# A higher queue priority for the attention steps of the second layer, on ScalarE and VectorE

## The chip, the cores and the metric

The kernel runs on one core of one Trainium2 chip. The time is the device time of one execution in microseconds (us). Three runs of the kernel before gave 984.35, 983.63 and 985.03, with a median of 984.35. The engines are named as in the profile: PE (TensorE matmul), PEld (its weight loads), DVE (VectorE), ACT (ScalarE), POOL (GpSimd), SP (SyncE, which issues most DMAs).

## The reference

A decoder trunk of two layers works on 16 learned meta tokens and 512 tokens of width 1024. The first layer is gated linear attention. The second layer, in which the change lies, is differential softmax attention with 8 heads. All is in float32. Cut to what matters:

```python
def diff_branch(xn, w_in, lam_vecs, gnorm, w_out, rel_table, lambda_init):
    proj = xn @ w_in                                  # 1024 -> 4 * 2048
    q, k, v, z = jnp.split(proj, 4, axis=-1)
    ...
    def block(args):                                  # 128 queries, all heads
        s = jnp.einsum('bhpqd,bhpkd->bhpqk', qb, kh) * scale + bias[None, :, None]
        s = jnp.where(dist >= 0, s, -jnp.inf)
        p = jax.nn.softmax(s, axis=-1)
        a = p[:, :, 0] - lam * p[:, :, 1]             # two softmaxes per head
        return jnp.einsum('bhqk,bhkv->bhqv', a, vh)
    ...
    o = head_rms(o) * gnorm.astype(f32) * (1.0 - lambda_init)
    y = jax.nn.silu(z.astype(f32)) * o.reshape(B, L, D_INNER)
    return (y.astype(xn.dtype) @ w_out)
```

After both layers a final RMS norm is taken and the meta tokens are dropped.

## The kernel before

**Precision.** Every float32 product is made of three matmuls of a shortened type: high times high, high times low, low times high. So each operand is split: `split` lets ACT copy the value into the shortened type (line 269, the high part), and DVE subtract that from the value (line 270, the low part). Weights come from DRAM into tiles called `raw` and are split into `wh`, `wl`.

**Projection units.** For queries, keys, values and gates of a head the weights are taken in 2 x 2 blocks, and a `Unit` multiplies with sums of blocks, so that fewer products are needed. Its block weights are `a11h`, `a11l`, `a12h` and so on, its sums of weights `sum` (line 356). Each product goes into one of the PSUM banks `bx`, `bv`, `by` (line 421, `product`). The first product and one in the middle are evacuated by ACT into a tile `u` (line 442, `partial`); later products are added to `u` by DVE into `t` (lines 467 and 469, `add`). There are two banks `bx` and one each of the others: until `u` or `t` has emptied a bank, PE cannot begin the product that takes it next.

**Attention of a head.** `diff_steps` returns four steps, each for one of four blocks of 128 queries. `scores` makes the two score products on PE (line 390), adds the bias tile `T` on DVE and keeps the minimum of the negated scores (line 1635), takes the exponentials on ACT (line 1637, tile `p`) and joins the two softmaxes on DVE (lines 1640 to 1642). `turn` transposes the result on PE and splits it into `aT` and, for the 16 meta keys, `am` (ACT lines 269, 397, 398; DVE lines 270, 400). `values` multiplies with the values on PE (lines 390 and 1666) and takes the head's RMS norm: ACT (lines 1670, 1671), a power on POOL (line 1673), ACT again (line 1674, tile `on`). `rows` transposes that on PE (line 1680), multiplies with the gate on DVE (line 1683, tile `yt`) and splits it into `hT`.

Values must be reversed in token order: `leave` copies them into `planes` (line 579), sends them to DRAM (line 580), and transposing DMAs on SP bring them back (lines 588, 590).

**What sets the order.** PE's list is written out by hand: the whole kernel is under a manual schedule for PE, so PE's instructions run in the order of the code. In the second layer the code is a loop over heads and steps; after each step a planner `W` fills in pieces of projection units for the next head until a share of their time is used up. So the code's order interleaves one head's attention with the next head's projections. For ACT, DVE and SP a scheduler builds the lists: among the instructions it holds ready in its own model, the one of the highest priority goes first. The priority follows the place in the code; `high_priority(offset=...)` moves an instruction ahead as if it stood that many places earlier. The helper `urgent` gives 100 to what it wraps: the four attention steps, `partial`, `add`, `gate` (lines 1514 to 1516) and `leave`. Splits of weights have no such offset.

Of the kernel before, what the change touches and what calls it, by code (L numbers as in the profile page):

```python
# [208 lines left out]
def trunk(ctx, tc, x, meta, g_norm, gla_w_in, gla_w_gate_up, gla_b_gate, gla_gnorm, gla_w_out,  # L209
# [21 lines left out]
    def T(p, shape, dt, tag, **kw):  # L231
        uid[0] += 1
        return p.tile(shape, dt, tag=tag, name=f"{tag}_{uid[0]}", **kw)
# [10 lines left out]
    def ps_tile():  # L244
        return T(ps_pool, [P, 512], F32, "ps")
# [4 lines left out]
    def h2(t):  # L250
        return t.rearrange("p (a b) -> p a b", a=2)

    def urgent(fn):

        def run(*a, **kw):
            with tc.high_priority(offset=100):
                return fn(*a, **kw)
        return run


    kept = []

    def split(hi, lo, src, scale=None, keep=False):

        if keep:
            act.activation(hi, src, AF.Copy)
            kept.append(lambda: dve.tensor_tensor(lo, src, hi.bitcast(F32), op=ALU.subtract))
        elif scale is None:
            act.activation(hi, src, AF.Copy)  # L269
            dve.tensor_tensor(lo, src, hi.bitcast(F32), op=ALU.subtract)  # L270
        else:
            act.activation(hi, src, AF.Copy, scale=scale)
            dve.scalar_tensor_tensor(lo, src, scale, hi.bitcast(F32), op0=ALU.mult, op1=ALU.subtract)
# [112 lines left out]
    def mm3(ps, a, b, first=True, last=True, **kw):  # L386

        pairs = ((a[0], b[0]), (a[0], b[1]), (a[1], b[0]))
        for n, (l, r) in enumerate(pairs):
            pe.matmul(ps, l, r, start=first and n == 0, stop=last and n == 2, **kw)  # L390

    def split3(dst, src, lo, scale=None):


        kw = {} if scale is None else {"scale": scale}
        hi = dst[:32].bitcast(F32)
        act.activation(dst[:32], src, AF.Copy, **kw)
        act.activation(dst[96 - lo:128 - lo], src, AF.Copy, **kw)
        if scale is None:
            dve.tensor_tensor(dst[lo:lo + 32], src, hi, op=ALU.subtract)  # L400
        else:
            dve.scalar_tensor_tensor(dst[lo:lo + 32], src, scale, hi, op0=ALU.mult, op1=ALU.subtract)
# [873 lines left out]
    pf = ps_tile()  # L1276
    pe.matmul(pf[0:1, 0:1], fl[:, 1:2], one1, start=True, stop=True)
    told = urgent(dve.tensor_copy)(fi, pf[0:1, 0:1])
    with tc.issue_after(told.ins):
        token_sums(4)  # L1280
# [68 lines left out]
    def boundary(m):  # L1349
        urgent(split)(xs2[0][m], xs2[1][m], hT[:, m, :], scale=g_sb[:, 1, m:m + 1])  # L1350
        if m >= 4:
            squares2(m)

        def post():
            if m == 0:
                bd.pm = ps_tile()
            pt = ps_tile()
            for b in range(4):
                pe.transpose(pt[:, b * P:(b + 1) * P], hT[:, m, NM + b * P:NM + (b + 1) * P], ident)
            if m < 4:  # L1360
                pe.transpose(bd.pm[:NM, m * P:(m + 1) * P], hT[:, m, :NM], ident)
            act.activation(hacc[:, :, m * P:(m + 1) * P], pt.rearrange("p (b c) -> p b c", b=4), AF.Copy)
            if m == 3:
                for b in range(5):
                    n = BLK[b][1]
                    t = hacc[:, b - 1, :512] if b else bd.pm[:NM, :]
                    act.activation(tmp()[:n, :512], t, AF.Square, accum_out=sums[:n, b:b + 1])
        W.defer(2.6, post)
        if m == KT - 1:
            W.defer(2.8, norm_sums)  # L1370
# [66 lines left out]
    for i in range(2):  # L1437
        urgent(dve.tensor_tensor)(z0r[:, i, :], z0[i], rb[:, NM:], op=ALU.mult)
# [179 lines left out]
    def diff_steps(hd, s, ys):  # L1618


        @urgent
        def scores(b):
            r = Head()
            r.nk = nk = NM + P * (b + 1)
            r.ta, r.b = b * P, b
            r.st = st = T(ep, [P, 8], F32, "st", bufs=4)
            r.p = []
            ko = L - nk
            for m in range(2):
                p = T(ep, [P, L], F32, "p", bufs=3)  # L1630
                for c0, c1 in ([(0, nk)] if nk <= 512 else [(0, HT), (HT, L)]):
                    ps = ps_tile()
                    mm3(ps[:, :c1 - c0], [s.q[j][:, m, r.ta:r.ta + P] for j in range(2)],
                        [s.k[j][:, m, ko + c0:ko + c1] for j in range(2)])
                    dve.tensor_tensor_reduce(p[:, c0:c1], ps[:, :c1 - c0], s.T[:, c0:c1], op0=ALU.add, op1=ALU.min, scale=1.0,  # L1635
                                             scalar=st[:, m:m + 1] if c0 else 1.0e38, accum_out=st[:, m:m + 1])
                act.activation(p[:, :nk], p[:, :nk], AF.Exp, scale=-1.0, bias=st[:, m:m + 1], accum_out=st[:, 2 + m:3 + m])  # L1637
                r.p.append(p[:, :nk])

            dve.reciprocal(st[:, 5:6], st[:, 3:4])  # L1640
            dve.scalar_tensor_tensor(st[:, 5:6], st[:, 5:6], lam, st[:, 2:3], op0=ALU.mult, op1=ALU.mult)
            dve.scalar_tensor_tensor(r.p[0], r.p[1], st[:, 5:6], r.p[0], op0=ALU.mult, op1=ALU.subtract)
            return r

        @urgent
        def turn(r):
            b, a = r.b, r.p[0]
            pt, pm = ps_tile(), ps_tile()
            for j in range(b + 1):
                pe.transpose(pt[:, j * P:(j + 1) * P], a[:, j * P:(j + 1) * P], ident)  # L1650
            pe.transpose(pm[:32, :P], a[:, r.nk - 32:r.nk], ident)
            r.am = T(ep, [M3, P], F32R, "am", bufs=1)
            r.aT = [T(ep, [P, 512], F32R, f"aT{i}", bufs=1) for i in range(2)]
            w = (b + 1) * P
            split(r.aT[0][:, :w], r.aT[1][:, :w], pt[:, :w])
            split3(r.am, pm[:32, :P], 64)

        @urgent
        def values(r):
            b = r.b  # L1660
            ps = ps_tile()
            po = ps[:, :256]
            for j in range(b + 1):
                mm3(po, [r.aT[i][:, j * P:(j + 1) * P] for i in range(2)],
                    [s.v[i][:, b - j, :] for i in range(2)], j == 0, False)
            pe.matmul(po, r.am, s.vm, start=False, stop=True)  # L1666

            r.on = T(ep, [P, 257], F32, "on")
            ms = r.st[:, 6:7]
            act.activation(ps[:, 256:257], r.st[:, 2:3], AF.Copy, scale=16.0 * math.sqrt(EPS))  # L1670
            act.activation(r.on, ps[:, :257], AF.Square, scale=1.0 / 16, accum_out=ms)  # L1671
            r.on = r.on[:, :256]
            pool.tensor_tensor(ms, ms, mhalf[:, :1], op=ALU.pow)  # L1673
            act.activation(r.on, po, AF.Copy, scale=ms)

        @urgent
        def rows(r):
            pt = ps_tile()
            for m in range(2):
                pe.transpose(pt[:, m * P:(m + 1) * P], r.on[:, m * P:(m + 1) * P], ident)  # L1680
            y = T(ep, [P, 2, P], F32, "yt")
            cs = slice(r.ta, r.ta + P)
            W.mark = dve.tensor_tensor(y, pt[:, :256].rearrange("p (m c) -> p m c", m=2), s.z[:, :, cs], op=ALU.mult)
            split(ys[hd][0][:, :, cs], ys[hd][1][:, :, cs], y)

        R = {}

        def A(b):
            R[b] = scores(b)

        return A, lambda b: turn(R[b]), lambda b: values(R[b]), lambda b: rows(R[b])

    def want_last(hd):
# [185 lines left out]
def build(shapes):  # L1879
    import concourse.bacc as bacc  # L1880

    nc = bacc.Bacc("TRN2", target_bir_lowering=False, num_devices=1, dynamic_dma_scratch_size=512)
    args = [nc.dram_tensor(f"in_{n}_dram", shp, F32, kind="ExternalInput").ap() for n, shp in shapes]
    args.append(nc.dram_tensor("out_0_dram", (1, NR, D), F32, kind="ExternalOutput").ap())
    with tile.TileContext(nc) as tc:
        trunk(tc, *args)
    return nc
# [15 lines left out]
```

## Time and profile before

| from the profile | value |
|---|---|
| time of the profiled execution | 984.03 us |
| its span, first to last instruction | 982.3 us |
| granted TensorE clock, mean | 0.999 |
| PE busy | 967.6 us (99%), 7065 matmuls |
| DVE busy | 777.2 us (79%) |
| ACT busy | 616.2 us (63%) |
| POOL busy | 50.8 us (5%) |
| DMA | 96.27 MB, mean 98 GB/s |

A row of the timeline gives the start in us from the span's start, the duration in us, the engine, the line of the code, the operation, out<-in by the names of the tiles (numbers left out), the size, and how many like instructions in a row it stands for. Behind it, in brackets, stands how long the engine was idle before, and what ended that. A row of the waits gives the waiting instruction, what it waited for, and then the sum in us, the number of waits and the longest. Durations of pipelined matmuls overlap: what a matmul adds is read from one start to the next.

The second layer's heads follow each other from about 519 us to the end.

### The profile page before, as it was taken

How to read it: one execution, taken by the hardware profiler on the slowest of the kernel's cores; microseconds unless marked ns; L12 is line 12 of the kernel's file. 1: busy time of each engine (PE TensorE's matmuls, PEld its weight loads, DVE VectorE, ACT ScalarE, POOL GpSimd, SP SyncE). 2: the span in 40 equal slices, each digit the busy share in tenths (PEclk: the TensorE clock that was granted, in tenths of full speed). 3: DMA queues.
4: the chain of work that ended last, by engine and by line, in shares of the span. 5: the costliest groups of instructions: out<-in, count | busy, mean ns of one | idle time of the engine just before them, and what ended most of it. 6: DMA issues, size and time to landing. Idle time of an engine off the chain costs nothing. (4 is left out here: it accounts for less than half of the span.)

```text
span 982.3 us, 18166 instructions
## 1 busy us (share of the span) xinstructions
PE 967.6 (99%) x7065; PEld 914.7 (93%) x7065; DVE 777.2 (79%) x1584; ACT 616.2 (63%) x1306; POOL 50.8 (5%) x68
## 2 busy tenths in 40 slices
PE   9999999999999999999999999999999999999997
PEld 8999999998999999999999998898998999989896
DVE  7899985887778787556998885977968879677785
ACT  7775755575546566536657675566764667655573
POOL 1000000000000000000001001001010000000001
PEclk9999999999999999999999999999999999999999
DMA  7322224621362222122322514234252251612212
GB/s 194 87 86 67 69 81 134 143 87 43 109 162 87 86 87 86 45 85 87 97 87 79 155 63 139 75 98 136 86 147 86 87 146 46 187 56 86 86 65 86
DMA packets 108490, 96.27 MB, mean 98 GB/s; under 512 B 33117, under 2 KB 94845, under 8 KB 108400
## 3 DMA queue, kind: packets, MB, share of 16 engines
q1 hardware_dynamic: 105520, 89.61, 30.7%
q10 hardware_dynamic: 2880, 5.46, 1.6%
q8 instruction: 57, 0.93, 0.4%
q14 instruction: 33, 0.27, 0.1%
HBM read 83.64 MB, written 7.57 MB: 93 GB/s over the span
## 5 line engine op out<-in xcount | busy, mean ns | idle before, releaser
L270 DVE TENSOR_TENSOR wl<-raw,wh 128x1024 fp32r<-128x1024 f32 x98 | 119.5, 1221 | 26.2 <-ACT wh L269 17.9
L269 ACT ACTIVATE wh<-raw 128x1024 fp32r<-128x1024 f32 x98 | 103.1, 1054 | 54.1 <-PE by L957 26.5
L421 PE MATMUL bv<-x,wh 128*128 128x264 f32 (+1 forms) x656 | 97.6, 287 | 0.6 <-DVE z L469 0.6
L421 PE MATMUL bx<-x,wh 128*128 128x264 f32 (+1 forms) x640 | 95.2, 286 | 0.5 <-ACT u L442 0.3
L421 PEld LDWEIGHTS bv<-x,wh 128*128 128x128 f32 x656 | 86.3, 189 | 1.2 <-DVE z L469 0.8
L421 PEld LDWEIGHTS bx<-x,wh 128*128 128x128 f32 x640 | 84.5, 188 | 1.7 <-ACT u L442 0.9
L270 DVE TENSOR_TENSOR wl<-sum,wh 128x1024 fp32r<-128x1024 f32 x41 | 50.1, 1222 | 17.6 <-ACT wh L269 15.7
L442 ACT ACTIVATE u<-bx 128x264 f32<-128x264 f32 (+1 forms) x120 | 45.4, 379 | 28.3 <-PE bx L421 24.9
L411 PE MATMUL bx<-x,wh 128*128 128x512 f32 (+1 forms) x256 | 62.5, 386 | 0.0
L1673 POOL TENSOR_TENSOR st<-st,mhalf 128x1 f32<-128x1 f32 x32 | 31.6, 987 | 465.4 <-ACT on L1671 447.2
L421 PE MATMUL bv<-x,wl 128*128 128x264 f32 (+1 forms) x328 | 55.2, 285 | 0.1
L421 PE MATMUL bx<-x,wl 128*128 128x264 f32 (+1 forms) x320 | 53.9, 285 | 0.0
L1637 ACT ACTIVATE p<-p,st 128x528 f32<-128x528 f32 (+3 forms) x64 | 36.4, 569 | 24.8 <-DVE st L1635 24.3
L411 PEld LDWEIGHTS bx<-x,wh 128*128 128x128 f32 x256 | 44.5, 188 | 7.9
L269 ACT ACTIVATE wh<-sum 128x1024 fp32r<-128x1024 f32 x41 | 43.2, 1054 | 12.3 <-PE bv L421 4.1
L421 PE MATMUL by<-x,a12h 128*128 128x264 f32 (+1 forms) x320 | 46.5, 285 | 0.0
L421 PE MATMUL bx<-x,a11h 128*128 128x264 f32 (+1 forms) x320 | 46.5, 285 | 0.0
L421 PEld LDWEIGHTS bv<-x,wl 128*128 128x128 f32 x328 | 45.9, 188 | 0.4 <-issue 0.3
L421 PEld LDWEIGHTS bx<-x,wl 128*128 128x128 f32 x320 | 45.0, 188 | 0.6 <-DVE wl L270 0.5
L269 ACT ACTIVATE a11h<-raw 128x512 fp32r<-128x512 f32 x41 | 25.8, 628 | 31.1 <-DMA raw<-in_diff_w_in_dram 15.8
L421 PEld LDWEIGHTS bx<-x,a11h 128*128 128x128 f32 x320 | 42.3, 188 | 0.8
L421 PEld LDWEIGHTS by<-x,a12h 128*128 128x128 f32 x320 | 41.7, 188 | 0.0
(479 smaller groups left out, 2639.4 us busy)
## 6 DMA issues: line engine op xcount, KB each, us to landing
raw<-in_gla_w_in_dram SPq DMA_DIRECT2D x48, 512.0 KB, 3.9
raw<-in_diff_w_in_dram SPq DMA_DIRECT2D x42, 512.0 KB, 4.6
raw<-in_diff_w_in_dram SPq DMA_DIRECT2D x11, 1024.0 KB, 5.7
raw<-in_gla_w_out_dram SPq DMA_DIRECT2D x8, 1024.0 KB, 5.2
raw<-in_diff_w_out_dram SPq DMA_DIRECT2D x8, 1024.0 KB
vd<-planes ACTq DMA_DIRECT2D x12, 268.0 KB, 3.0
vd<-keep ACTq DMA_DIRECT2D x8, 264.0 KB, 2.3
T<-bdr SPq DMA_DIRECT2D x8, 264.0 KB, 3.6
```

Of the source, the lines that this page charges most:

```text
L269: act.activation(hi, src, AF.Copy)
L270: dve.tensor_tensor(lo, src, hi.bitcast(F32), op=ALU.subtract)
L411: pe.matmul(bank, a[:, k, :], b[k] if n0 is None else b[k][:, n0 + i * nn:n0 + (i + 1) * nn], start=n == 0 and ks[0] == 0, stop=n == len(t ...
L421: pe.matmul(bank[:, :x[q].shape[2]], w[p][:, k * P:(k + 1) * P], x[q][:, k, :], start=first and i == 0, stop=i == len(PASSES) - 1, skip_gr ...
L442: W.moved = act.activation(t, self.bx[:, :self.n], AF.Copy, scale=self.sc)
L1637: act.activation(p[:, :nk], p[:, :nk], AF.Exp, scale=-1.0, bias=st[:, m:m + 1], accum_out=st[:, 2 + m:3 + m])
L1673: pool.tensor_tensor(ms, ms, mhalf[:, :1], op=ALU.pow)
```

## The change

`urgent` takes the offset as an argument, and a new helper `soonest` gives 170. The four steps of `diff_steps` are wrapped in `soonest` in place of `urgent`. `partial`, `add`, `gate` and `leave` stay at 100.

```diff
-    def urgent(fn):
+    def urgent(fn, offset=100):
 
         def run(*a, **kw):
-            with tc.high_priority(offset=100):
+            with tc.high_priority(offset=offset):
                 return fn(*a, **kw)
         return run
+
+    def soonest(fn):
+        return urgent(fn, 170)
...
     def diff_steps(hd, s, ys):
-        @urgent
+        @soonest
         def scores(b):
...
-        @urgent
+        @soonest
         def turn(r):
...
-        @urgent
+        @soonest
         def values(r):
...
-        @urgent
+        @soonest
         def rows(r):
```

No instruction is added or removed. PE's and POOL's lists are the same. ACT's list differs in 18 places, DVE's in 13 and SP's in 2 (a bias tile that is loaded behind a piece of weights and no longer ahead of it), all in the second layer. Lines of the changed kernel behind the helper are three higher: line 442 is 445 there.

The first place is ACT at the scores of the first block of head 1, about 564 us. `u` with input `bx` is an evacuation of a projection unit; `p` are the two exponentials of 128 x 528. Before:

```order
L397 ACTIVATE vm_9334<-lands_9742,short 32x256
L398 ACTIVATE vm_9334<-lands_9742,short 32x256
L442 ACTIVATE u_9856<-bx_9775 128x256
L1637 ACTIVATE p_9823,st_9822<-p_9823,st_9822 128x528
L1637 ACTIVATE p_9835,st_9822<-p_9835,st_9822 128x528
L269 ACTIVATE wh_9873<-sum_9792 128x1024
```

The same place in the changed kernel:

```order
L400 ACTIVATE vm_9334<-lands_9742,short 32x256
L401 ACTIVATE vm_9334<-lands_9742,short 32x256
L1640 ACTIVATE p_9823,st_9822<-p_9823,st_9822 128x528
L1640 ACTIVATE p_9835,st_9822<-p_9835,st_9822 128x528
L445 ACTIVATE u_9856<-bx_9775 128x256
L272 ACTIVATE wh_9873<-sum_9792 128x1024
```

The evacuation moved behind both exponentials.

The second place is ACT beside the last values product of a block of head 5, about 793 us. Before:

```order
L579 ACTIVATE planes_12617<-t_12519 128x1072
L580 DMA vd_12618<-planes_12617 128x1072 x2
L269 ACTIVATE hT_8837<-yt_12652 128x2x128
L442 ACTIVATE u_12665<-bx_12574 128x264
L1670 ACTIVATE ps_12674<-st_12228 128x1
L269 ACTIVATE wh_12693<-raw_12475 128x1024
L1671 ACTIVATE on_12682,st_12228<-ps_12674 128x257
L269 ACTIVATE a11h_12871<-raw_12861 128x512
L1674 ACTIVATE on_12682<-ps_12674,st_12228 128x256
L442 ACTIVATE u_12709<-bx_12574 128x264
```

The same place in the changed kernel:

```order
L582 ACTIVATE planes_12617<-t_12519 128x1072
L272 ACTIVATE hT_8837<-yt_12652 128x2x128
L583 DMA vd_12618<-planes_12617 128x1072
L1673 ACTIVATE ps_12674<-st_12228 128x1
L583 DMA vd_12618<-planes_12617 128x1072
L1674 ACTIVATE on_12682,st_12228<-ps_12674 128x257
L445 ACTIVATE u_12665<-bx_12574 128x264
L1677 ACTIVATE on_12682<-ps_12674,st_12228 128x256
L272 ACTIVATE wh_12693<-raw_12475 128x1024
L272 ACTIVATE a11h_12871<-raw_12861 128x512
L445 ACTIVATE u_12709<-bx_12574 128x264
```

The first `u` moved behind L1670 and L1671 of the block (1673 and 1674 in the new numbers), which read what PE's L1666 completes, and the split of a weight moved behind L1674 (now 1677), which waits for POOL's power. At 665 us (head 3) the order is changed in the same way, with the first `u` behind `hT` and L1670 only, and the second `u` behind L1674 and a weight split.

The third place is DVE at a block of head 7, about 911 us. `k` are the low parts of the next keys, `aT` and `am` the low parts of the turned scores. Before:

```order
L270 TENSOR_TENSOR wl_14052<-raw_13722,wh_14051 128x1024
L270 TENSOR_TENSOR k_2537_13978<-t_13980,k_2536_13977 128x512
L270 TENSOR_TENSOR k_2537_13978<-t_13980,k_2536_13977 128x16
L270 TENSOR_TENSOR k_2537_13978<-t_13979,k_2536_13977 128x512
L270 TENSOR_TENSOR k_2537_13978<-t_13979,k_2536_13977 128x16
L270 TENSOR_TENSOR aT_2559_14084<-ps_14078,aT_2558_14083 128x128
L400 TENSOR_TENSOR am_14082<-ps_14079,am_14082 32x128
L1683 TENSOR_TENSOR yt_14099<-ps_14096,z_13087 128x256
```

The same place in the changed kernel:

```order
L273 TENSOR_TENSOR wl_14052<-raw_13722,wh_14051 128x1024
L273 TENSOR_TENSOR k_2537_13978<-t_13980,k_2536_13977 128x512
L273 TENSOR_TENSOR aT_2559_14084<-ps_14078,aT_2558_14083 128x128
L403 TENSOR_TENSOR am_14082<-ps_14079,am_14082 32x128
L273 TENSOR_TENSOR k_2537_13978<-t_13980,k_2536_13977 128x16
L273 TENSOR_TENSOR k_2537_13978<-t_13979,k_2536_13977 128x512
L1686 TENSOR_TENSOR yt_14099<-ps_14096,z_13087 128x256
L273 TENSOR_TENSOR k_2537_13978<-t_13979,k_2536_13977 128x16
```

`aT` and `am` moved ahead of three of the four `k` pieces.

At the last block of heads 0 and 1 (about 533 and 586 us) the split of a weight that the same unit uses next (`wh` on ACT, `wl` on DVE) moved from behind the two copies of line 579 and the two exponentials to ahead of them.

## The prediction

> **What bounds the kernel now.** I read the page's first part, then PE's waits between 519 and 960 us, the stretch in which the change moves anything, then the timelines where a moved instruction stands near a PE instruction that needs it.
>
> ```profile
> PE 967.6 (99%) x7065; PEld 914.7 (93%) x7065; DVE 777.2 (79%) x1584; ACT 616.2 (63%) x1306; POOL 50.8 (5%) x68
> ```
> ```profile
> PE ps L390 <- DVE aT L270: 0.7, 1, 0.7
> PE ps L1680 <- ACT on L1674: 0.7, 1, 0.7
> PE bx L421 <- ACT u L442: 0.3, 1, 0.3
> ```
>
> PE is busy 99% of the span; its list is the same before and after. The change can only pay by shortening PE's waits, and these three make 1.7 us in all. It can only cost by making new ones: wherever an evacuation or a split moves back by more than the time between its end and the matmul that needs it. So I price sites, not sums of busy time. ACT and DVE run their lists in the listed order in this trace, so an instruction that is put behind others ends later by their start-to-start times, or when the last of them has got what it waits for.
>
> **The change, site by site.** Most of the moved instructions end further ahead of the matmul that needs them than they move back; they cost nothing, because PE has other matmuls queued meanwhile. Eight sites are left.
>
> *Head 1, 564 us.* The first shown piece: u goes behind the two exponentials.
>
> ```profile
> 564.10 0.39 ACT L442 ACTIVATE u<-bx 128x256 f32<-128x256 f32 x1
> 564.38 0.73 ACT L1637 ACTIVATE p<-p,st 128x528 f32<-128x528 f32 x1
> ...
> 565.10 0.72 ACT L1637 ACTIVATE p<-p,st 128x528 f32<-128x528 f32 x1
> ```
> ```profile
> 563.83 0.08 DVE L1635 DVE_READ_ACCUMULATOR2_ANT st<- 128x1 f32 x1
> ```
> ```profile
> 564.83 1.11 PE L421 MATMUL bx<-x,wh 128*128 128x256 f32 x8
> ```
>
> Both exponentials have their input by 563.91 (the DVE row), so they take u's place at 564.10 and step by 0.72 (564.38 to 565.10). u starts at 564.10 + 1.44 = 565.54 and ends at 565.93. PE's eight matmuls into the bank that u empties start at 564.83 today; they will start at 565.93: +1.10. Nothing behind them is free to run sooner, since PE keeps its order.
>
> A wait on PE also costs a little after it. The four matmuls behind the wait at 591.33 take 0.76, an undisturbed four 0.65 (795.06 below). I add 0.10 per new wait: **+1.20**.
>
> *Head 5, 793 us.* The second shown piece: u goes behind L1670, a DMA issue and L1671.
>
> ```profile
> 793.24 0.42 ACT L269 ACTIVATE hT<-yt 128x256 fp32r<-128x256 f32 x1 [0.41 <-ACT planes L579]
> 793.56 0.37 ACT L442 ACTIVATE u<-bx 128x264 f32<-128x264 f32 x1
> ...
> 794.87 0.37 ACT L1671 ACTIVATE on<-ps 128x257 f32<-128x257 f32 x1
> ```
> ```profile
> 793.19 0.28 PE L1666 MATMUL ps<-vm,am 96*128 96x256 f32 x1
> ...
> 794.04 1.18 PE L421 MATMUL bx<-x,wh 128*128 128x264 f32 x8
> 795.06 0.65 PE L421 MATMUL bx<-x,wl 128*128 128x264 f32 x4
> ```
>
> L1670 needs PE's L1666, which ends at 793.47; it takes 0.17 (row of 666.36 below), the DMA issue about 0.3 beside it, and L1671 0.27 to 0.37 more, so u ends at about 794.67 and PE starts at about 794.69 instead of 794.04: +0.65, with the restart **+0.75**.
>
> *Head 3, 665 us.* The same move: u behind hT and L1670.
>
> ```profile
> 665.35 0.39 ACT L442 ACTIVATE u<-bx 128x264 f32<-128x264 f32 x1 [0.41 <-ACT planes L579]
> 665.63 0.41 ACT L269 ACTIVATE hT<-yt 128x256 fp32r<-128x256 f32 x1
> 666.36 0.17 ACT L1670 ACTIVATE ps<-st 128x1 f32<-128x1 f32 x1 [0.32 <-PE ps L1666]
> ```
> ```profile
> 666.04 0.29 PE L1666 MATMUL ps<-vm,am 96*128 96x256 f32 x1
> 666.16 1.15 PE L421 MATMUL bx<-x,wh 128*128 128x264 f32 x8
> ```
>
> L1670 still waits for L1666 (666.33), so u runs from about 666.45 to 666.86, and PE's matmuls start at 666.88 instead of 666.16: +0.72. But the same block of attention holds PE up 14 us later, and that wait may go:
>
> ```profile
> 677.64 2.58 POOL L1673 TENSOR_TENSOR st<-st,mhalf 128x1 f32<-128x1 f32 x1 [8.46 <-ACT on L1671]
> ```
> ```profile
> 679.13 0.68 DVE L270 TENSOR_TENSOR a22l<-raw,a22h 128x512 fp32r<-128x512 f32 x1
> ```
> ```profile
> 680.78 0.44 PE L1680 MATMUL ps<-ident,on 128*128 128x128 f32 x2 [0.68 <-ACT on L1674]
> ```
> ```profile
> 899.82 0.55 POOL L1673 TENSOR_TENSOR st<-st,mhalf 128x1 f32<-128x1 f32 x1 [10.85 <-ACT on L1671]
> 668.01 1.18 POOL L1673 TENSOR_TENSOR st<-st,mhalf 128x1 f32<-128x1 f32 x1 [10.09 <-ACT on L1671]
> ```
>
> The power on POOL takes 0.55 where DVE idles (899.82) and 2.58 here; it ends at 680.22, 0.41 after DVE's unbroken run of subtractions (last row, end 679.81). After the change, L1671 of the block before is ahead of a 1.04 us split, its power falls into idle DVE time, L1674 and what follows on ACT come some 0.8 earlier, and the run with them; the power would end near 679.3 and PE would need its result at 680.66. The wait, 0.84 by starts, goes: +0.72 - 0.84 = **-0.12**. Bounds: -0.12, and +0.82 if the wait stays and a restart is paid. I take the lower, since DVE's run starts from the aT of that block, which the new order brings forward.
>
> [...]
>
> *Head 7, 911 us.* The third shown piece: aT and am go ahead of three of the four k pieces.
>
> ```profile
> 910.99 1.46 DVE L270 TENSOR_TENSOR k<-t,k 128x512 fp32r<-128x512 f32 x4
> 912.36 0.28 DVE L270 TENSOR_TENSOR aT<-ps,aT 128x128 fp32r<-128x128 f32 x1
> ```
> ```profile
> 912.70 0.38 PE L390 MATMUL ps<-v,aT 128*128 128x256 f32 x1 [0.69 <-DVE aT L270]
> ```
>
> The pieces are two of 0.68 and two of 0.17 whose starts lie 0.60 and 0.09 apart (together 1.37, to 912.36). After one of them aT starts at 911.60, 0.76 earlier, and ACT's half of it is done by then (it ends at 911.23). PE moves by the same: **-0.76**. The k pieces are wanted by the next head's scores, far away.
>
> *Heads 0 and 1, 539 and 591 us.* The last split of the turned values' weights goes from behind two copies and two exponentials to ahead of them.
>
> ```profile
> 590.12 1.18 PE L421 MATMUL bx<-x,wh 128*128 128x264 f32 x8
> 591.33 0.76 PE L421 MATMUL bx<-x,wl 128*128 128x264 f32 x4
> ```
> ```profile
> 539.01 0.76 PE L421 MATMUL bx<-x,wl 128*128 128x264 f32 x4
> ```
>
> Eight matmuls are followed after 1.21 here, after 1.02 at 794.04: 0.19 of waiting, and 0.11 of restart: **-0.30**. At 539.01 only the restart shows, 0.76 against 0.65: **-0.11**. What goes behind the split, the copies, their DMAs and transposes and u, comes 1 to 2 us later: the copies are for the next head, and u keeps ahead of PE by the order of the list.
>
> *Head 7, 906 us.* yt goes ahead of t on DVE.
>
> ```profile
> 905.66 0.43 DVE L467 SCALAR_TENSOR_TENSOR t<-bv,u 128x264 f32<-128x264 f32 x1
> 906.00 0.41 DVE L1683 TENSOR_TENSOR yt<-ps,z 128x256 f32<-128x256 f32 x1
> ```
> ```profile
> 906.23 1.15 PE L421 MATMUL bv<-x,wh 128*128 128x264 f32 x8
> ```
>
> t ends 0.34 to 0.41 later than 906.09, PE starts 0.14 after that today: +0.25, with the restart **+0.35**.
>
> *Head 0, 535 to 552 us, and SP.* With that split earlier, SP issues half a weight load at about 535.3 instead of 539, ahead of the bias tile; the splits of that load stand ahead of attention's steps on ACT and DVE.
>
> ```profile
> 540.54 0.47 ACT L1674 ACTIVATE on<-ps,st 128x256 f32<-128x256 f32 x1 [1.32 <-POOL st L1673]
> ...
> 542.88 0.63 ACT L269 ACTIVATE a11h<-raw 128x512 fp32r<-128x512 f32 x1 [0.59 <-DMA raw<-in_diff_w_in_dram]
> ```
> ```profile
> raw<-in_diff_w_in_dram SPq DMA_DIRECT2D x42, 512.0 KB, 4.6
> ```
>
> At the median of 4.6 it lands at 539.9, and ACT, free at 538.7, stands for 1.2 with L1671 behind the split. Bounds 0 and +1.2. I take **0**: ACT idles 1.32 + 0.59 in these rows, which the moved work fills. The bias tile is for the next head.
>
> **Sum.** 1.20 + 0.75 + 0.35 - 0.12 - 0.76 - 0.30 - 0.11 = +1.01 on the profiled execution's 984.03. That lies 0.32 below the median of the runs, 984.35, on which I forecast **985.4**. About 0.2%, 1.97 us, is what a measurement of this kernel tells from no change: this is inside.
>
> **Rivals.** *Slower: the power on POOL holds ACT with evacuations behind it.* At 668 and 795 the next u now stands behind L1674, which waits for the power. With 2.58 instead of 0.55, u and the add behind it come late: at 795 the add ends near 799.95 against 799.34 needed (+0.6), at 668 near 672.0 against 671.5 (+0.5), and the wait at 680 stays (+0.94). It begins to cost at a power of about 2.0, and passes 0.2% at about 2.3. Sum: 1.01 + 2.04 = +3.05, 987.4. For it: only the run at 680 shows what stretches the power. Against it: 1.18 at 668 under one split.
>
> *No effect.* The sites stay below the runs' scatter because the late evacuations turn out covered: 984.3. Against it: the waits above already hold one of 0.3 on a u, so this evacuation is not covered everywhere.
>
> *Faster: attention's steps were what PE waited for.* The waits at 591, 680, 912 and 539 go, 0.30 + 0.84 + 0.76 + 0.11 = 2.0, and the evacuations are covered: 982.3. Against it: at 564 two exponentials of 0.72 cannot fit into the time that u has.
>
> **How the numbers follow.** Forecast 0.52 (own range 984.2 to 986.3: it takes in +0.9 if the wait at 680 stays, and half of each late u); power on POOL, or head 0's load at its upper bound with the wait at 680 staying (+1.01 + 1.2 + 0.94 = +3.15, 987.5), 0.27; no effect 0.11; faster 0.10. Same is forecast and no effect, 0.63; slower 0.27; faster 0.10. The range from 983.2 to 988.0 leaves the faster case and the far end of the slower one out.
>
> **What would show it.** In the changed profile: a PE wait of about 1.1 on u of L442 near 564 and about 0.7 near 667 and 794; the wait on aT near 912 down to about 0.1; no wait on L1674 near 681; powers near 668 and 795 of about 0.55. Wrong would make it: a late weight load at 539 that reaches PE, or a PE wait at a site that I took as covered.

## The result and the profile after

The changed kernel takes 987.87 us (median of 7 runs, 987.14 to 988.84). The kernel before, run in the same comparison, takes 985.00 (7 runs, 983.63 to 985.36). The ratio is 1.0033 with a 95% interval from 1.0023 to 1.0042: slower by 0.33%, some 2.9 us. The forecast was 985.4 and no measurable change.

The profiled execution of the changed kernel took 987.14 us, its span is 985.4 us (before 982.3), its clock 0.998. The first two lines below are from its page (busy time, then the DMA issues with their median from issue to landing). The others are PE's waits between 519 and 965 us.

```profile
PE 967.5 (98%) x7065; PEld 913.9 (93%) x7065; DVE 777.7 (79%) x1584; ACT 615.4 (62%) x1306; POOL 48.2 (5%) x68
...
raw<-in_diff_w_in_dram SPq DMA_DIRECT2D x42, 512.0 KB, 4.8
```
```profile
PE bx L424 <- ACT u L445: 3.1, 5, 1.0
PE ps L1683 <- ACT on L1677: 1.2, 2, 0.7
PE ps L393 <- DVE aT L273: 0.4, 1, 0.4
PE ps L393 <- DVE yt L1686: 0.2, 1, 0.2
PE bv L424 <- DVE t L470: 0.2, 1, 0.2
```

Busy times are as before; PE's waits went from 1.9 us in four rows to 5.1 us in five. (The prediction shows three of the four; the fourth is 0.2 for `yt`, near 894, and it is there after the change too.) Most of it is now waiting for `u`, as forecast. Of the rest, `on` waits at two places, of which the one at 683 was there before, and `aT` at a place where it did not wait before.

These are the waits in the timeline of the changed kernel. Two that hardly changed are left out: `yt`, and a wait of 0.33 on `u` at 695 (0.35 before).

```profile
550.23 0.44 PE L1683 MATMUL ps<-ident,on 128*128 128x128 f32 x2 [0.45 <-ACT on L1677]
...
552.01 0.39 PE L393 MATMUL ps<-v,aT 128*128 128x256 f32 x1 [0.41 <-DVE aT L273]
...
563.59 0.65 PE L424 MATMUL bx<-x,wl 128*128 128x256 f32 x4
564.07 1.11 PE L424 MATMUL bv<-x,wh 128*128 128x256 f32 x8
565.02 0.64 PE L424 MATMUL bv<-x,wl 128*128 128x256 f32 x4
566.66 1.21 PE L424 MATMUL bx<-x,wh 128*128 128x256 f32 x8 [1.00 <-ACT u L445]
...
668.50 1.25 PE L424 MATMUL bx<-x,wh 128*128 128x264 f32 x8 [0.57 <-ACT u L445]
...
683.27 0.44 PE L1683 MATMUL ps<-ident,on 128*128 128x128 f32 x2 [0.71 <-ACT on L1677]
...
797.65 1.23 PE L424 MATMUL bx<-x,wh 128*128 128x264 f32 x8 [0.95 <-ACT u L445]
...
823.38 0.97 PE L424 MATMUL bx<-x,wh 128*128 128x256 f32 x6 [0.20 <-ACT u L445]
...
910.38 1.24 PE L424 MATMUL bv<-x,wh 128*128 128x264 f32 x8 [0.15 <-DVE t L470]
```

A wait by starts is 0.16 longer than its bracket. At 566.66: from 565.02 to 566.66 are 1.64, four such matmuls without a wait take 0.48 (563.59 to 564.07), so PE lost 1.16. To that comes a restart, here 0.10. The table counts all this by the start of every matmul around the place, in both executions. The prediction named the heads 3, 5 and 7 counted from one, and the heads 0 and 1 by the loop's index; the experiments below use the index throughout, so that its heads 3, 5, 7 are index 2, 4, 6 there.

| place | forecast | measured |
|---|---|---|
| index 1, 564: `u` behind two exponentials | +1.20 | +1.26 |
| index 4, 793: `u` behind L1670, a DMA issue, L1671 | +0.75 | +1.07 |
| index 2, 665: `u` behind `hT` and L1670 | +0.72 | +0.83 |
| the same block's wait at 680 | -0.84 | +0.05 |
| index 6, 911: `aT`, `am` ahead of `k` | -0.76 | -1.15 |
| index 1, 591, and index 0, 539: the split earlier | -0.41 | -0.50 |
| index 6, 906: `t` behind `yt` | +0.35 | +0.40 |
| index 0, 535 to 552 | 0 | +1.66 |
| index 5, 820, not among the sites | 0 | +0.25 |
| sum | +1.01 | +3.87 |

The profiled execution came to the second layer 0.85 us earlier than that of before (the like matmul starts at 519.20 and 520.05), a difference from the first layer, which the change does not touch. By every matmul of PE's list the second layer costs 3.94 (what the table leaves out is below 0.1 at each place), and 3.94 less 0.85 is the 3.1 of the spans.

The medians, over seven runs each, lie 2.87 apart, 1 us less than the sum. In a second profile of the changed kernel (below) the wait at 680 is gone, and the same count gives 2.9 (span 2.4 longer, second layer begun 0.45 earlier). How often the wait at 680 is there among the runs is not known.

### The profile page after: what moved, and what is told of

It reads as the page before. It is cut to its first block, busy times and chain, and to the rows that moved or that the text cites. A ratio compares the mean times of both kernels' runs of the same rounds, so it can differ in the third digit from the quotient of the medians.

```text
span 985.4 us, 18170 instructions
## 1 busy us (share of the span) xinstructions
PE 967.5 (98%) x7065; PEld 913.9 (93%) x7065; DVE 777.7 (79%) x1584; ACT 615.4 (62%) x1306; POOL 48.2 (5%) x68
## 5 line engine op out<-in xcount | busy, mean ns | idle before, releaser
L1676 POOL TENSOR_TENSOR st<-st,mhalf 128x1 f32<-128x1 f32 x32 | 29.0, 906 | 471.9 <-ACT on L1674 415.5
```

## The experiments

The first theory was that the prices of the moved evacuations hold, and that what the sum lacked comes from head 0: half of a weight load lands late there, and the splits of it stand ahead of attention's steps on ACT and DVE. Its part 1a says why the half is late: SP issues the bias tile between the two halves. Rivals were that head 0's waits come from the order on ACT and DVE alone, whatever the load does; and that the loss is made of something that all heads share.

In all diffs below the changed kernel stands on the minus side. Where a helper `step` was added, lines behind it are one higher (L1677 is L1678).

**Head 0 alone.** Only the steps of head 0 get the higher priority.

```diff
     def diff_steps(hd, s, ys):
+        step = soonest if hd in (0,) else urgent
...
-        @soonest
+        @step
         def scores(b):
```

(and the same for the other three steps)

> The higher priority in head 0 alone (loop index), the other heads at 100. Theory 1 (a split of a weight load that has not landed stands ahead of attention on ACT and DVE): PE's four new waits between 550 and 553 us of the changed kernel, 0.61, 0.58, 0.20 and 0.10, all come back, the restart of 0.11 at 539 goes, and the time is 1.4 above the kernel before (0.14%). Theory 2 (head 0's waits follow from something that the whole change does, and the late evacuations u of heads 1, 2 and 4 are all of the loss): no new wait near 550, time within 0.3 of before.

Measured: 986.09 (10 runs) against 984.41 (19 runs), ratio 1.0018, interval 1.0008 to 1.0027, so about +1.7 us; more than half of the whole loss. The rows are first those of the changed kernel, then those of this run: what SP issues, and what ACT, DVE and PE do about it.

```profile
534.44 0.37 SPq L294 DMA_DIRECT2D raw<-in_diff_w_in_dram  x1
535.23 0.34 SPq L1501 DMA_DIRECT2D T<-bdr  x1
535.62 0.43 SPq L294 DMA_DIRECT2D raw<-in_diff_w_in_dram  x1
...
538.69 0.63 ACT L272 ACTIVATE a11h<-raw 128x512 fp32r<-128x512 f32 x1 [1.16 <-DMA raw<-in_diff_w_in_dram]
...
543.09 0.63 ACT L272 ACTIVATE a12h<-raw 128x512 fp32r<-128x512 f32 x1 [2.13 <-DMA raw<-in_diff_w_in_dram]
543.63 0.37 ACT L272 ACTIVATE aT<-ps 128x256 fp32r<-128x256 f32 x1
...
543.03 0.69 DVE L359 TENSOR_TENSOR sum<-raw 128x512 f32<-128x512 f32 x1 [2.26 <-DMA raw<-in_diff_w_in_dram]
544.03 0.43 DVE L273 TENSOR_TENSOR aT<-ps,aT 128x256 fp32r<-128x256 f32 x1 [0.30 <-ACT aT L272]
```
```profile
534.85 0.37 SPq L294 DMA_DIRECT2D raw<-in_diff_w_in_dram  x1
...
536.02 0.43 SPq L294 DMA_DIRECT2D raw<-in_diff_w_in_dram  x1
...
543.35 0.69 DVE L359 TENSOR_TENSOR sum<-raw 128x512 f32<-128x512 f32 x1 [2.07 <-DMA raw<-in_diff_w_in_dram]
...
550.54 0.44 PE L1684 MATMUL ps<-ident,on 128*128 128x128 f32 x2 [0.44 <-ACT on L1678]
...
552.32 0.38 PE L393 MATMUL ps<-v,aT 128*128 128x256 f32 x1 [0.42 <-DVE aT L273]
```

The first half is used 4.25 us after its issue and ACT waits 1.16 for it, as the prediction's upper bound had it. The second half is used 7.4 us after its own issue (535.62 to 543.03), by DVE, which had waited for it. ACT and DVE then stand for another 2.1 and 2.3 with `aT` and `am` of attention queued behind. Without the change ACT makes `aT` at 541.49 and takes this half later. The three waits of the full change (0.61, 0.58 and 0.20 by starts, and 0.10 of restart) are all here, with no other head changed.

**Head 0 alone, and no bias tile between the halves.**

```diff
-                    heads[hd + 1].T = bias_tile(hd + 1)
+                    heads[hd + 1].T = bias_tile(hd + 1) if hd else s.T
```

> As the run of head 0 alone, but head 1's bias tile is not loaded (head 1 uses head 0's, so its scores are not the reference's); that DMA stood between the two halves of the weight load on SP. Every other list is the same. Theory 1a (the bias tile between the halves makes the second half late): ACT's wait of 2.1 us for the second half falls below 1.0 and PE's waits near 550 to 553 from 1.5 to below 0.6. Theory 1b (the load is late whatever stands between, because the copies of the values go out at the same time): ACT still waits about 2 us and PE about 1.5.

Measured: 984.29 in one profiled execution, span 982.5 (head 0 alone: 983.9).

```profile
534.79 0.92 SPq L294 DMA_DIRECT2D raw<-in_diff_w_in_dram  x2
...
541.94 0.69 DVE L359 TENSOR_TENSOR sum<-raw 128x512 f32<-128x512 f32 x1 [0.64 <-DMA raw<-in_diff_w_in_dram]
...
542.53 0.37 ACT L272 ACTIVATE aT<-ps 128x256 fp32r<-128x256 f32 x1
...
549.87 0.39 PE L1684 MATMUL ps<-ident,on 128*128 128x128 f32 x2
...
550.79 0.52 PE L393 MATMUL ps<-v,aT 128*128 128x256 f32 x3
```

Both halves are issued in one go, the second is used 7.15 after the first's issue in place of 8.50 to 8.59, and PE waits for neither `on` nor `aT`. What is left on PE is 0.08 at `am`, and 0.10 behind it. All other lists are those of the run before. So the order of ACT and DVE alone costs about 0.2 at head 0. The rest of head 0's loss (1.66 in the full change) needs the second half to land later still, and that later part, some 1.4 us, comes from the bias tile of 264 KB: without it the half's issue ends at 535.71 in place of 536.45, and from there to its use it takes 6.2 in place of 6.9. For the remaining lateness theory 1b, the copies of the values that go out at the same time, is not refuted. Even without the tile the half is used 6.2 us after the end of its issue (535.71 to 541.94), where the first half in the run before took 4.0 (535.22 to 539.19, where ACT had waited for it); why is open.

**Indices 2 and 4 alone.** The helper's line reads `hd in (2, 4)`.

> The higher priority in heads 2 and 4 alone. Theory 1: a PE wait on u of about 0.74 (and 0.1 behind it) near 666 us and one of 1.1 (and 0.1) near 795 us, the wait on L1674 near 681 us stays at about 0.85, the one near 820 us grows from 0.11 to about 0.36; in all +2.1 to +2.3 against the kernel before. Theory 3 (these waits in the changed kernel came from delays handed on by heads 0 and 1): near 0.3 at either u, and the wait near 820 us as before.

Measured: 985.96 in one profiled execution, span 984.2.

```profile
667.59 0.63 PE L424 MATMUL bx<-x,wh 128*128 128x264 f32 x3 [0.57 <-ACT u L445]
...
679.28 0.69 POOL L1677 TENSOR_TENSOR st<-st,mhalf 128x1 f32<-128x1 f32 x1 [10.69 <-ACT on L1675]
...
794.03 1.08 ACTq L583 DMA_DIRECT2D vd<-planes  x1
795.15 0.39 ACT L1675 ACTIVATE on<-ps 128x257 f32<-128x257 f32 x1 [0.96 <-ACT ps L1674]
...
795.96 1.25 PE L424 MATMUL bx<-x,wh 128*128 128x264 f32 x8 [1.25 <-ACT u L445]
```

The wait on `u` at 667 is as in the full change (0.73), the one at 796 is longer (1.41, there 1.11). Both stand here without any change in heads 0 and 1, so they are not handed on from there. The wait at 680 is gone, as the prediction had wanted it, with a power of 0.69, against what was expected for this run. At 796 the rows show what the wait is made of: the second DMA issue of `vd` takes 1.08 of ACT's time (0.79 in the full change, below), and L1675, then `u`, start only behind it.

```profile
796.01 0.79 ACTq L583 DMA_DIRECT2D vd<-planes  x1
796.84 0.39 ACT L1674 ACTIVATE on<-ps 128x257 f32<-128x257 f32 x1 [0.67 <-ACT ps L1673]
```

The prediction had 0.3 for that issue, beside L1670. In the three profiles with this order (the second one of the changed kernel stands below) the issue took 0.72, 0.79 and 1.08 and the wait on `u` 1.05, 1.11 and 1.41, so the one follows the other. Why it takes 0.34 in the trace of before and 0.72 to 1.08 here is open.

**The evacuation raised with the steps.** The whole change, and `partial` too at 170, so that it keeps its old place among the steps.

```diff
-        @urgent
+        @soonest
         def partial(self)
```

> The changed kernel with the evacuation u (partial) at 170 as well, so that u stands ahead of attention again at 564, 665 and 793 us. Theory 1: the three PE waits on u of 1.2, 0.7 and 1.1 go with the 0.1 behind each, head 0's 1.5 stays, so the time lies 3.2 below the changed kernel and 0.5 above the kernel before, 0.05%. Theory 4 (an attention priority above weight splits and adds costs by itself, wherever u stands): still 2 or more above the kernel before.

Measured: 985.18 (10 runs), ratio to before 1.0008, interval 0.9996 to 1.0020. That cannot be told from the kernel before. The medians lie 0.8 above the kernel before here and 2.9 above it for the changed kernel, so raising `partial` takes back about 2.1 us. The waits on `u` at 566, 667 and 796 are gone, so these three were made by the order of `u` against the steps. Head 0's wait stays, nearly all in one piece:

```profile
552.65 0.44 PE L1683 MATMUL ps<-ident,on 128*128 128x128 f32 x2 [1.08 <-ACT on L1677]
```

**The evacuation raised, head 0 as before.** The edit above, and the helper's line `step = urgent if hd == 0 else soonest`.

> The evacuation u at 170 with the attention steps, and head 0's steps left at 100 as in the kernel before. Theory 1 (late u of three heads and the late weight load of head 0 are the loss; the gains at 591 and 912 us are real): no PE wait near 550 to 553, none on u near 566, 667 and 795, none on aT near 912; the time lies 1.4 below the run with u at 170 alone and 0.5 to 1.0 below the kernel before (0.05 to 0.1%). Theory 4 (the higher priority costs wherever it acts): above the kernel before.

Measured: 982.61 (11 runs, 981.43 to 983.96) against 984.39 (21 runs), ratio 0.9982, interval 0.9973 to 0.9991: faster than the kernel before by about 1.8 us; the changed one is slower than it by 2.9. Theory 4 is refuted: the higher priority does not cost wherever it acts. PE's larger waits in its profile are these.

```profile
PE ps L1684 <- ACT on L1678: 1.5, 1, 1.5
PE bx L424 <- ACT u L445: 0.4, 1, 0.4
```

The gains at 591 and 912 are kept. Two costs are left: `t` near 906 (0.19 and 0.09 behind it), and 681, where the power on POOL takes 3.16 in this profile and PE waits 1.65 by starts, 0.81 more than before. With that wait the profiled execution gains only 0.5 by the spans (981.8 and 982.3). The median gains more; a power that is short in other runs would explain it, but that is not shown.

**Only `turn` of index 6.** `turn` is at 170 in that head alone; everything else is as before.

> The higher priority for the step turn of head 6 alone. Theory 1: the waits on aT and am near 912 us (0.85, 0.20 and 0.10 behind them) go and nothing else in the second layer changes by over 0.15, so -1.1 against the kernel before, 0.11%. Rival: PE stands for the next instruction that attention delays, yt or hT behind aT, and less than 0.5 is gained.

Measured: 983.93 (11 runs), ratio 0.9996, interval 0.9987 to 1.0005, in the same comparison as the run before this one. PE's wait on `aT` at 912 is gone but for 0.08, and the one on `am` behind it is left (0.20 by starts): 0.77 gained in place of 1.15. The gain cannot be told from nothing by the times; the medians lie 0.46 apart.

**The changed kernel once more.** No edit.

> The changed kernel once more, for a second profile. If the power of head 2 (near 680 us) gets in between two DVE instructions by a chance of some tens of ns, it may take 0.7 here instead of 2.55 and the PE wait of 0.87 near 683 is gone; if the order alone decides it, 2.55 and 0.87 again. All other PE waits above 0.15 stay within 0.05, except the one on u near 797 us, which follows the length of a DMA issue on ACT (0.79 in the first profile).

Measured: 986.48 in one profiled execution, span 984.7. Every wait of the table is there again within 0.1 us, but one: at 680 there is none. Outside the table, the wait on `u` at 695 is 0.23 shorter, and of the 0.12 that head 0 lost near 545 in the first profile 0.04 is left. First the rows of the first profile of the changed kernel, then those of this one; the program is the same.

```profile
679.72 0.77 DVE L273 TENSOR_TENSOR k<-t,k 128x512 fp32r<-128x512 f32 x2
680.41 0.69 DVE L273 TENSOR_TENSOR a12l<-raw,a12h 128x512 fp32r<-128x512 f32 x1
...
681.61 0.69 DVE L273 TENSOR_TENSOR a22l<-raw,a22h 128x512 fp32r<-128x512 f32 x1
680.16 2.55 POOL L1676 TENSOR_TENSOR st<-st,mhalf 128x1 f32<-128x1 f32 x1 [10.66 <-ACT on L1674]
```
```profile
679.89 0.80 DVE L273 TENSOR_TENSOR k<-t,k 128x512 fp32r<-128x512 f32 x2
680.61 0.68 DVE L273 TENSOR_TENSOR a12l<-raw,a12h 128x512 fp32r<-128x512 f32 x1
...
680.33 0.70 POOL L1676 TENSOR_TENSOR st<-st,mhalf 128x1 f32<-128x1 f32 x1 [10.51 <-ACT on L1674]
```

The power starts 0.44 after `k` in both. In the first profile it lasts until DVE's run is over (682.30, and 0.41 more). In the second it is done in 0.70, and `k` with the next subtraction behind it takes 0.72 from start to start in place of 0.69. The same step of 0.72 stands beside the short power of the run with indices 2 and 4 alone (678.83 to 679.55, the power 0.69). So in this order the wait at 680 differs from execution to execution. What decides it is not shown: the starts of the power differ by 0.01 at most, and the 0.03 between the two subtractions can be the cause of the short power or its effect.

**Indices 1 and 6 alone.** The helper's line reads `hd in (1, 6)`.

> The higher priority in heads 1 and 6 alone. Theory 1: a PE wait on u of 1.16 (and 0.1) near 566 us; no wait near 591 (0.30 gone); the waits near 912 (1.15) gone; a wait of 0.31 (and 0.1) on t near 908; in all +0.2 against the kernel before. Theory 3 (handed on from head 0): no wait above 0.3 near 566.

Measured: 983.61 in one profiled execution, span 981.8 (before 982.3). The wait on `u` at 565.17 is 1.17, that at 591 is gone, and all of the 912 site is gone (-1.15). The wait at 565 stands here without head 0, so it is not handed on from there. The wait on `t` at 906.83 is 0.13 in place of the 0.31 expected. The balance of these two heads is about nothing: what this part of the change gives at 591 and 912 it takes back at 565 and 907. At 681 the old order stands, and the power takes 2.58.

**Indices 3, 5 and 7 alone.** The helper's line reads `hd in (3, 5, 7)`.

> Only the attention steps of the heads with loop index 3, 5 and 7 have the higher priority; the heads 0, 1, 2, 4 and 6, where all the priced sites lie, are as in the kernel before. Two readings of the wait near 820 us, which the full change grew from 0.11 to 0.36 and 0.45, and which stands in the steps of the head with index 5. If the moved instructions of head 5 make it, it is 0.3 to 0.5 here and the span 0.2 to 0.4 longer than the 982.3 of before. If it comes from a weight load near 796 us that lands later in head 4's changed order (DVE's run of subtractions ahead of 820 then starts later), it is 0.11 here as before. In both readings the waits of before stay (591: 0.3, 681: 0.8 to 1.1, 912: about 1.1) and nothing new stands at 550, 566, 667 or 796; the span is 982.0 to 982.8 (0.11 at 820) or 982.4 to 983.0.

Measured: 985.30 in one profiled execution, span 983.5; the like matmul at the start of the second layer stands 0.9 us later than in the profile of before (520.96 and 520.05), and that is nearly all of the longer span. At 820.93 the wait is 0.11, as before. So the moved instructions of index 5 do not make the growth at 820. A wait of 0.29 at 800 appeared instead, in the old order of index 4, where a weight half landed late (ACT waits 1.85 for it, 1.56 in the profile of before):

```profile
798.25 0.63 ACT L272 ACTIVATE a11h<-raw 128x512 fp32r<-128x512 f32 x1 [1.85 <-DMA raw<-in_diff_w_in_dram]
```

The full change shows 0.36 and 0.45 at 820 in its two profiles, indices 2 and 4 alone show 0.11. In the full change the load issued near 794 lands later (ACT waits 1.65 for it, 0.71 with indices 2 and 4 alone), and DVE's run of subtractions up to 820 starts later. That fits, but it was not isolated: this term, 0.25 us, stays open.

## Why the prediction was wrong

**The step that failed** is the one on head 0: "Bounds 0 and +1.2. I take **0**: ACT idles 1.32 + 0.59 in these rows, which the moved work fills." It measured +1.66, of which 1.54 is the three waits at 550 to 552 and their restarts, and 0.12 stands near 545. The bounds were worked out from the landing of the first half of the weight load. That half did land about when the prediction said, and ACT did stand for 1.16. That wait is not the cost: without the bias tile it is there too, at 1.32, and PE loses 0.2. The cost came from the second half, which was never priced: SP issues it behind the bias tile, it lands at 543.0 and not with the first, and its split too stands ahead of `aT` and `am`. The prediction says itself that "half a weight load" goes ahead of the bias tile, and sets the tile aside ("The bias tile is for the next head"); it does not ask where that leaves the other half. The run without the bias tile between the halves shows this: same order on ACT and DVE, and 0.2 on PE in place of the 1.54.

**The second step that failed** is the wait at 680, counted at -0.84, measured +0.05 in the first profile and gone in the second. "I take the lower, since DVE's run starts from the aT of that block, which the new order brings forward": the run did not come forward. In both orders `aT` on ACT stands behind a12h, and a12h waits for a weight load, first in the kernel before, then in the changed one:

```profile
670.69 0.63 ACT L269 ACTIVATE a12h<-raw 128x512 fp32r<-128x512 f32 x1 [0.48 <-DMA raw<-in_diff_w_in_dram]
671.22 0.26 ACT L269 ACTIVATE aT<-ps 128x128 fp32r<-128x128 f32 x1
```
```profile
673.28 0.63 ACT L272 ACTIVATE a12h<-raw 128x512 fp32r<-128x512 f32 x1 [2.02 <-DMA raw<-in_diff_w_in_dram]
673.82 0.26 ACT L272 ACTIVATE aT<-ps 128x128 fp32r<-128x128 f32 x1
```

By 673 PE is about 2.5 behind the profile of before, and a12h starts 2.59 later: the load sets its start. ACT came to it earlier against PE, and only waited longer, 2.02 in place of 0.48. DVE's run ends at 682.30, 2.49 later than the 679.81 of before, and the power starts 2.52 later. That the wait is gone in other executions is the power's doing, and not a run that came forward; counting it at -0.84 came true there by luck.

Both failed steps have this in common: attention stands behind the split of a weight load, and the load's landing was not worked out. At head 0 only one half was priced, by the median of all such loads; at 680 none was.

The account also starts from "these three make 1.7 us in all", which leaves out the fourth row, 0.2 on `yt`. The change does not touch that wait, so nothing of the sum hangs on it. At 820 the prediction took 0 and 0.25 came.

**Right in mechanism, mis-sized.** Index 4's `u`: +0.75 forecast, +1.07 measured, because the DMA issue on ACT that it stands behind took 0.79 and not 0.3 (a wait of 1.11 and a restart of 0.06, less a restart of 0.10 nearby that went). Index 6's `aT`: -0.76 forecast, -1.15 measured; `am` (0.20) and the restart (0.10) went as well, and `aT` was there in time in full (0.85).

**Right.** `u` behind two exponentials (+1.20, measured +1.26), `u` at index 2 (+0.72, +0.83), the earlier split (-0.41, -0.50), `t` behind `yt` (+0.35, +0.40). The run with `partial` raised shows that the three waits on `u` come from its place in the list.

**The rivals.** The power on POOL as a holder of evacuations did not come: the powers near 668 and 797 took 0.55.

```profile
668.95 0.55 POOL L1676 TENSOR_TENSOR st<-st,mhalf 128x1 f32<-128x1 f32 x1 [9.42 <-ACT on L1674]
...
797.45 0.55 POOL L1676 TENSOR_TENSOR st<-st,mhalf 128x1 f32<-128x1 f32 x1 [9.16 <-ACT on L1674]
```

DVE idles at both (it starts its next instruction at 669.80 and 799.48, after 2.49 and 3.41 of idle time). So 0.55 stands beside an idle DVE here, as at 899.82 in the profile of before. At 680, beside DVE's run of subtractions, the power took 2.55 in the first profile of the changed kernel, 0.70 in the second, 0.69 with indices 2 and 4 alone and 3.16 with `partial` raised and head 0 as before. What sets its length there is not shown.

The case nearest to what came is the other one that shares the 0.27 with the power: "head 0's load at its upper bound with the wait at 680 staying", 987.5 against the 987.87 measured. That it comes so close is in part luck. Its 1.2 was for the first half, and the measured cost came from the second; and the wait at 680 stayed in one profile of two. "No effect" fell with the waits on `u`; "faster" fell with them too, but the gains that it counted at 591 and 912 are real, and the run with `partial` raised and head 0 left as before collects them. Its 982.61 is near the 982.3 worked out for "faster", but that sum counted the waits at 539 and 680 too; the one at 539 stays there, and the one at 680 is longer in its profile.

## What to carry to other kernels

A higher priority for one chain can be paid by whoever empties the banks that the busiest engine fills next. Here it was, with waits of 1.16, 0.73 and 1.11 us on `u`; raising the evacuations with it took those waits away. Before a step is moved ahead on a queue, price every transfer whose landing it depends on by that transfer's own issue, piece by piece; here the second half of a load was used 8.50 to 8.59 us after the first's issue with the bias tile issued between the halves, and 7.15 without it. Where a priority helps in some places and hurts in one, give it by place: with the evacuations raised, head 0 alone took back all that the other heads gave (0.8 above the kernel before with it, 1.8 below without).

## What the runs showed of the hardware

- A power of 128 x 1 on POOL beside DVE's run of subtractions took 2.55 in one execution of a program and 0.70 in another. In the six profiles whose order at this place is that of the kernel before, it was long every time, 2.56 to 2.58. Where the order was the changed one, it took 2.55, 0.70 and 0.69, and with `partial` raised as well 0.69 and 3.16.
- A DMA issue on ACT took 0.34 to 0.45 at most places, and 0.72, 0.79 and 1.08 at one place in the three profiles with the changed order there. It held back the next instruction of ACT's list there, which started 0.04 to 0.05 after its end each time.
- Of a weight load issued in two halves of 512 KB with a transfer of 264 KB issued in between, the second half was used 8.50 to 8.59 us after the first's issue, and 7.15 without that transfer.
- After most waits on another engine PE lost 0.06 to 0.11 more, one matmul after the wait: in the first profile of the changed kernel the first step behind the waits on `u` is 0.22 to 0.23, and the next ones are 0.12.
